# A hybrid encoder block on one core: two copies ahead of two subtractions, denser side steps at the end of the gates, a later Silu

## The chip, the cores and the metric

The kernel runs on one core of a Trainium2 chip. A core has five engines that the text speaks of: TensorE (PE in the profile, with PEld for its weight loads), VectorE (DVE), ScalarE (ACT), GpSimd (POOL) and SyncE (SP), which here issues nearly all DMAs. Each engine works off its own instruction queue strictly in order, and semaphores hold an instruction until what it needs is there. So an instruction that waits also holds everything that stands behind it on its engine. The metric is the time of one execution in microseconds of device time.

## The reference

The reference is one layer of a bidirectional hybrid encoder, with 1024 tokens of width 1024, all in fp32. What the change touches is in these lines, where `h` is the normalised input:

```python
proj = h @ w_in[l]
q, k, v, r, lr_f, lr_b, u, g_a, g_b = jnp.split(proj, split_points, axis=-1)
...
y_a = o @ w_branch_gla[l]            # o: gated linear attention of q, k, v, times silu(r)
...
merged = jax.nn.sigmoid(g_a) * y_a + jax.nn.sigmoid(g_b) * y_b     # y_b: pooling mixer of u
x = x + merged @ w_out[l]
h2 = rmsnorm(x, norm_ffn[l])
gate, up = jnp.split(h2 @ w_ffn_in[l], 2, axis=-1)
x = x + (jax.nn.silu(gate) * up) @ w_ffn_out[l]
```

## The kernel before

**Products.** Every fp32 operand is split into a high part (an fp32r cast by ACT) and a low part (what the cast lost, a subtraction on DVE or POOL). A product of one 128 by 512 tile and one k-tile is three matmuls: high with high, high with low, low with high (`products`, L268, and `mm3`, L273). The larger multiplications (the merge gates, branch and output projections, the FFN) are done in blocks of two by two with seven products in place of eight, so many sums and differences of blocks are formed first and split afterwards. One such product, in the gates and in the FFN, is twelve matmuls in a row into one bank of PSUM.

**The order of work** is written out by hand. The program issues TensorE's work in its order, and after each `mm3` calls `pump`, which counts the matmul time issued in units of one `mm3` of 512 columns and lets side work into the queues when its time has come:
- `soon(delay, step)` puts a step off by `delay` units;
- weights (`Ahead`, `Weights`) are split four products ahead: the cast `wh` on ACT (L197) and the low part `wl` on POOL (L198);
- `prepare_beside(jobs, every, put, lag)` takes a list of small jobs and does one step of it every `every` units. A step forms a sum or a difference on POOL (L636), casts the piece of an earlier step on ACT (`uph`, L630), subtracts for the piece before that on DVE (`upl`, L621), and puts the finished pair to DRAM on SP (L617). `finish_beside()` works off all steps that are left, at once. The `uph` and `upl` come from a ring of five buffers, so a cast waits until an earlier put has landed.

**The stages**, by the times of the trace: norms and the first transposes with the values of a pair of heads (to about 45 us); the first queries and keys and the attention of the four heads (to about 385); the merge gates (`Gates`, ten runs n = 0 to 9, to about 585); the branch projection, the merged projection (to 745); the FFN, whose first products run while the second half of the normalised input is still being transposed (`features(1)`, 744 to 788); FFN units and the output product (to 1381).

Three places matter here:
- `pair_products` (L440) forms the values of two heads at a time. A PSUM bank holds 256 columns for each head, and each half is split into `vh` and `vl`.
- At run n == 7 of the gates the side job is the splitting of the weights of the first two FFN units (`unit_jobs`, L563, two units, `READY`). In each of the last runs the pooled values of a group (`ph`, `pl`) are loaded (`load_pooled`, L1240) for the pooled product `yb`. The copies `ga` (ACT, L1308) take a finished product out of its bank, which TensorE needs again later.
- `features(half)` (L1525) transposes the normalised input, scales it into `hb` (ACT, L1540), and forms differences (DVE, L1554 and L1557) that are split into `gh` (ACT, `cast_block`, L1517) and `gl` (`low_block`, L1521, on DVE or POOL). Meanwhile `Gated.run` takes in the first gate products; for the first units the Silu of the gate is put off with `soon`.

Of the kernel before, what the change touches and what calls it, by code (L numbers as in the profile page):

```python
# [15 lines left out]
ALU = mybir.AluOpType  # L16
# [9 lines left out]
DV = 256  # L26
# [25 lines left out]
def kernel(  # L52
# [20 lines left out]
    nc = tc.nc  # L73
# [36 lines left out]
    def as_f32(ap):  # L110
        return ap.bitcast(F32)
# [39 lines left out]
    def soon(delay, *steps):  # L151
        put_off.extend([delay, step] for step in steps)
# [43 lines left out]
    def split_to(hi, lo, src, eng=nc.vector):  # L196
        nc.scalar.copy(hi, src)  # L197
        eng.tensor_tensor(lo, src, as_f32(hi), op=ALU.subtract)  # L198
# [239 lines left out]
    pair_v = [[], []]  # L438

    def pair_products(ts, before=None):  # L440
        banks = [bank(ps_mm) for _ in ts]
        for k in range(KT):
            if before:
                before(k)
            for ps, t in zip(banks, ts):
                mm3(ps[:, :], tokens(hT(k, t // 4), t), pair_w[k], k == 0, k == KT - 1)
        for ps, t in zip(banks, ts):
            for h in range(2):
                if t // 4 == len(pair_v[h]):
                    pair_v[h].append((slot(F32R, (4, DV), "vh"), slot(F32R, (4, DV), "vl")))  # L450
                split_to(*(part[:, t % 4, :] for part in pair_v[h][t // 4]), ps[:, h * DV : (h + 1) * DV])

    def first_steps(k):
        if k % 2 == 0:
# [68 lines left out]
    READY = 2  # L523
# [120 lines left out]
    def prepare_beside(jobs, every, put=PUT, lag=1):  # L644
        aside.append([beside(chain(*jobs), every, put, lag), every])

    def finish_beside():
        while aside:
            for _ in aside[0][0]:
                pass  # L650
            aside.pop(0)
# [250 lines left out]
    for h in range(HEADS):  # L902
# [7 lines left out]
        if h > 1:  # L910
            v = value_slots()
# [5 lines left out]
    class Unit:  # L917
# [14 lines left out]
        def block(self, i, j):  # L932
            return self.raw[i][:, 4 * j : 4 * j + 4, :]
# [227 lines left out]
    def load_block(i, j):  # L1161

        ob[i, j] = [slot(s="ob") for _ in range(2)]
        for c in range(2):
            nc.sync.dma_start(ob[i, j][c][:, :, :], ob_out[i, 1 - j][:, 2 * c : 2 * c + 2, :])
# [74 lines left out]
    def load_pooled(g):  # L1240

        while g not in stored and side:
            if next(side[0][0], None) is None:
                side.pop(0)
        if g not in stored:
            settle()
        pools[g] = [slot(F32R, s=s) for s in ("ph", "pl")]
        for n, t in enumerate(pools[g]):
            nc.sync.dma_start(as_f32(t[:, :, :]), p_out[g][n])
# [99 lines left out]
    for n, run in enumerate(gate_runs):  # L1349
        zs[n] = Gates(n)  # L1350
        last = n == len(gate_units) - 1
        if n == 0:
            prepare_beside(map(output_jobs, range(4)), 2.8)
        if n == 7:
            finish_side()
            finish_beside()
            prepare_beside(map(unit_jobs, range(READY)), 3.1, 1, 2)
        if last:
            finish_beside()
        for at, (of, p) in enumerate(run):  # L1360
            if not gates_ahead.step() and at in (5, 7):
                line_make()
            if n >= 6 and at == 2 and not last:
                load_pooled(n - 6)
            zs[of].run(p)
            for _ in range(2 * (at == 0 and not last)):
                gunits[n + 1].load()
            if p in (7, 4):
                zs[of].store(int(p == 4))
            if at == 4:  # L1370
                flush()
                if n == 2:
                    begin(pooling(), 4)
            if 5 <= n < 9 and at == 5:
                load_pool_weights(n - 5)
            elif n >= 6 and at == 2:
                split_pool_weights(n - 6)
            if n >= 6 and at == 0 and last:
                load_pooled(n - 6)
            if last and at == 1:  # L1380
                load_block(0, 0)
                line_load()
                line_load()
                load_block(1, 0)
            elif last and at == 2:
                line_load()
                line_load()
                load_block(0, 1)
                load_block(1, 1)
# [129 lines left out]
    def low_block(p, i, src, eng=nc.vector):  # L1519
        hi, lo = split_b[p][i]  # L1520
        eng.tensor_tensor(lo[:, :, :], src, as_f32(hi[:, :, :]), op=ALU.subtract)  # L1521
        if i == 1:
            split_done.add(p)

    def features(half):  # L1525

        for i in range(2):
            blocks[i, half] = [slot(s="hb") for _ in range(2)]

        def block(i, j, c):  # L1530
            return blocks[i, j][c][:, :, :]

        waiting = []
        for k in range(KT):
            ps = bank(ps_g, "tr")
            for i in range(4):
                nc.tensor.transpose(
                    ps[:, i * P : (i + 1) * P], xn[4 * half + i][:, k * P : (k + 1) * P], ident[:, :]
                )
            nc.scalar.activation(  # L1540
                blocks[k // 4, half][k % 4 // 2][:, k % 2, :], ps[:, :], AF.Copy, scale=g_ffn[:, k : k + 1]
            )
            if waiting:
                waiting.pop()()
            i = k % 4 // 2
            if k % 2 and half == 0:
                p, src = (1, block(0, 0, i)) if k < 4 else (2, block(1, 0, i))
                cast_block(p, i, src)
                low_block(p, i, src, nc.gpsimd)
            elif k % 2:  # L1550

                t = block(0, 0, i)
                if k < 4:
                    sub(t, block(0, 1, i), t)  # L1554
                    waiting.append(partial(cast_block, 5, i, t))
                else:
                    sub(t, block(1, 1, i), t)  # L1557
                    waiting.append(partial(cast_block, 6, i, t))
                    if k == KT - 1:
                        waiting.pop()()  # L1560
            elif half and k in (2, 4):
                low_block(5, k // 2 - 1, block(0, 0, k // 2 - 1), nc.gpsimd)
            elif half and k == 6:
                low_block(6, 0, block(0, 0, 0))
            yield 2 if half == 0 else 1.6 if k % 2 else 1.2
        if half == 0:
            return

        low_block(6, 1, block(0, 0, 1))
        for i in range(2):  # L1570
            cast_block(3, i, block(1, 1, i))
            yield 2.5
        for p, b in ((7, block(0, 1, 0)), (7, block(0, 1, 1)), (4, block(1, 0, 0)), (4, block(1, 0, 1))):
            i = len(split_b.get(p, ()))
            if p == 7:
                low_block(3, i, block(1, 1, i))
                sub(b, block(1, 1, i), b)
            else:
                low_block(7, i, block(0, 1, i))
                sub(b, b, block(0, 0, i))  # L1580
            cast_block(p, i, b)
            yield 3.5
        for i in range(2):
            low_block(4, i, block(1, 0, i))
# [70 lines left out]
    class Gated:  # L1655
# [15 lines left out]
        def run(self, p):  # L1671
            ps = bank_of(self, p)
            product(self.unit, p, ps, split_b)
            self.done.add(p)
            ps = ps[:, :]
            mul = partial(nc.vector.tensor_tensor, op=ALU.mult)
            if p == 1:
                self.sg = self.g[:, 0, :] if self.g else t2(s="sg")[:, :]
                nc.scalar.copy(self.sg, ps)  # L1679
            elif p == 2:  # L1680
                add(self.sg, ps, self.sg)  # L1681
                silu = partial(nc.scalar.activation, self.sg, self.sg, AF.Silu)
                if self.g:
                    soon(1, silu)
                else:
                    silu()
            elif p == 6:
                nc.scalar.copy(self.gate, ps)
            elif p == 5:
                nc.scalar.copy(self.up, ps)  # L1690
            elif p == 7:
                add(self.up, ps, self.up)
            elif p == 3:
                add(self.gate, ps, self.gate)
                nc.scalar.activation(self.gate, self.gate, AF.Silu)
            else:
                self.g = self.g or slot(s="g")
                mul(self.g[:, 0, :], ps, self.sg)
            if p in (3, 7) and {3, 7} <= self.done:
                self.g = self.g or slot(s="g")  # L1700
                mul(self.g[:, 1, :], self.gate, self.up)
# [255 lines left out]
```

## Time and profile before

| | us |
|---|---|
| median of 3 runs | 1389.14 |
| lowest and highest run | 1387.99, 1391.54 |
| profiled execution | 1389.97 |
| its span in the trace | 1388.2 |
| mean granted clock of TensorE | 0.998 |

By stage, the busy time of each engine, as the view by windows gives it:

| window | PE | DVE | ACT | POOL | DMA share |
|---|---|---|---|---|---|
| 0 to 40 | 32.16 | 25.50 | 26.64 | 13.95 | 0.58 |
| 40 to 140 | 98.67 | 46.94 | 52.22 | 24.76 | 0.17 |
| 140 to 385 | 243.95 | 159.00 | 141.08 | 90.01 | 0.31 |
| 385 to 585 | 197.72 | 126.91 | 89.60 | 133.98 | 0.79 |
| 745 to 788 | 40.38 | 26.33 | 24.89 | 10.27 | 0.47 |
| 788 to 1185 | 397.00 | 234.72 | 140.49 | 266.08 | 0.53 |
| 1185 to 1388.2 | 196.26 | 93.78 | 84.61 | 101.39 | 0.60 |

A row of the timeline reads: start, duration, engine, line, operation, what it writes and what it reads, shapes, how many such instructions in a row (x), and in brackets how long the engine had been idle before it and what ended that. Names are those of the tiles without buffer numbers. In the rows of the grouped waits the numbers are total idle time, how many times, and the longest.

### The profile page before, as it was taken

The numbers are of one execution on the slowest core, as the hardware profiler recorded it, in microseconds if no ns is written. First come the engines' busy times: TensorE is split into PE (matmuls) and PEld (weight loads), VectorE is DVE, ScalarE is ACT, GpSimd is POOL, SyncE is SP. The second block draws the span as 40 slices with busy tenths as digits, with TensorE's granted clock in tenths as the row PEclk, the third lists the DMA queues.
The fourth block names the chain that finished last, engine by engine and source line by source line (L and its number), as shares of the span: only waits on it lengthen the run. The fifth ranks groups of instructions, "written<-read, shape, count | busy, mean of one in ns | idle before, by whom it ended". The sixth has DMA issues, their size and how long they took to land. (4 is left out here: it accounts for less than half of the span.)

```text
span 1388.2 us, 18151 instructions
## 1 busy us (share of the span) xinstructions
PE 1366.0 (98%) x6485; PEld 1142.5 (82%) x6485; DVE 837.0 (60%) x1017; ACT 642.4 (46%) x1168; POOL 754.7 (54%) x557
## 2 busy tenths in 40 slices
PE   7999999999999999999999999999999999999997
PEld 6788898988888888788888788888888888888886
DVE  6364656557745875687883866565565556343374
ACT  6465766654334444554347533333333334444352
POOL 3222617132288645668665276666766667455453
PEclk9999999999999999999999999999999999999999
DMA  6112413312478677996516355555444447975551
GB/s 224 31 50 58 138 57 127 110 56 77 136 222 282 199 230 231 370 406 221 190 61 242 109 180 174 174 175 172 140 143 145 143 152 266 381 298 187 173 212 76
DMA packets 166586, 243.60 MB, mean 175 GB/s; under 512 B 10936, under 2 KB 95968, under 8 KB 166496
## 3 DMA queue, kind: packets, MB, share of 16 engines
q1 hardware_dynamic: 166352, 242.18, 51.6%
q8 instruction: 51, 0.84, 0.2%
q14 instruction: 39, 0.32, 0.1%
q10 hardware_dynamic: 144, 0.26, 0.0%
HBM read 164.55 MB, written 77.86 MB: 175 GB/s over the span
## 5 line engine op out<-in xcount | busy, mean ns | idle before, releaser
L198 POOL TENSOR_TENSOR wl<-fs,wh 128x512 fp32r<-128x512 f32 x120 | 167.1, 1396 | 149.5 <-ACT wh L197 100.4
L271 PE MATMUL ps<-gh,wh 128*128 128x512 f32 x616 | 240.7, 391 | 1.5 <-ACT gh L1517 0.8
L271 PE MATMUL ps<-gl,wh 128*128 128x512 f32 x616 | 240.0, 390 | 0.9 <-DVE gl L1521 0.9
L271 PE MATMUL ps<-gh,wl 128*128 128x512 f32 x616 | 239.7, 389 | 0.0
L198 POOL TENSOR_TENSOR wl<-fraw,wh 128x512 fp32r<-128x512 f32 x90 | 128.5, 1428 | 63.9 <-ACT wh L197 61.0
L271 PE MATMUL ps<-hh,wh 128*128 128x512 f32 x376 | 151.8, 404 | 0.0
L198 POOL TENSOR_TENSOR ol<-gor,oh 128x1024 fp32r<-128x1024 f32 (+1 forms) x42 | 101.0, 2408 | 86.4 <-ACT oh L197 62.0
L271 PE MATMUL ps<-hh,wl 128*128 128x512 f32 x376 | 146.9, 391 | 0.6 <-POOL wl L198 0.6
L271 PE MATMUL ps<-hl,wh 128*128 128x512 f32 x376 | 146.6, 390 | 0.0
L271 PEld LDWEIGHTS ps<-gh,wh 128*128 128x128 f32 x616 | 115.7, 188 | 26.4 <-ACT gh L1517 1.2
L271 PEld LDWEIGHTS ps<-gl,wh 128*128 128x128 f32 x616 | 115.7, 188 | 25.5 <-DVE gl L1521 1.6
L271 PEld LDWEIGHTS ps<-gh,wl 128*128 128x128 f32 x616 | 115.7, 188 | 24.0
L271 PE MATMUL ps<-oh,oh 128*128 128x512 f32 x308 | 119.8, 389 | 0.0
L271 PE MATMUL ps<-ol,oh 128*128 128x512 f32 x308 | 119.8, 389 | 0.0
L271 PE MATMUL ps<-oh,ol 128*128 128x512 f32 x308 | 119.8, 389 | 0.0
L198 POOL TENSOR_TENSOR wl<-raw,wh 128x512 fp32r<-128x512 f32 x40 | 54.5, 1373 | 118.2 <-ACT wh L197 109.6
L198 POOL TENSOR_TENSOR wl<-wraw,wh 128x512 fp32r<-128x512 f32 x56 | 91.9, 1672 | 42.3 <-ACT wh L197 39.4
L198 DVE TENSOR_TENSOR ol<-wor,oh 128x1024 fp32r<-128x1024 f32 (+1 forms) x42 | 61.9, 1486 | 66.9 <-ACT oh L197 54.3
L197 ACT CAST wh<-fs 128x512 fp32r<-128x512 f32 x120 | 73.8, 615 | 29.3 <-DVE fs L937 28.3
L271 PEld LDWEIGHTS ps<-hh,wl 128*128 128x128 f32 x376 | 70.6, 188 | 16.1 <-POOL wl L198 1.1
L271 PEld LDWEIGHTS ps<-hh,wh 128*128 128x128 f32 x376 | 70.7, 188 | 13.4 <-ACT wh L197 0.5
L271 PEld LDWEIGHTS ps<-hl,wh 128*128 128x128 f32 x376 | 70.8, 188 | 12.9
(259 smaller groups left out, 3120.9 us busy)
## 6 DMA issues: line engine op xcount, KB each, us to landing
fraw<-in_w_ffn_in_dram SPq DMA_DIRECT2D x44, 512.0 KB, 6.0
gor<-g_out SPq DMA_DIRECT2D x35, 512.0 KB, 5.0
g_out<-s SPq DMA_DIRECT2D x44, 256.0 KB, 2.3
raw<-in_w_in_dram SPq DMA_DIRECT2D x40, 256.0 KB, 4.8
fraw<-in_w_in_dram SPq DMA_DIRECT2D x20, 512.0 KB, 6.6
wor<-t_out SPq DMA_DIRECT2D x20, 512.0 KB
g_out<-g SPq DMA_DIRECT2D x33, 256.0 KB, 2.3
x<-in_x_dram SPq DMA_DIRECT2D x16, 512.0 KB, 4.1
```

The costliest lines, as they stand in the source:

```text
L197: nc.scalar.copy(hi, src)
L198: eng.tensor_tensor(lo, src, as_f32(hi), op=ALU.subtract)
L271: nc.tensor.matmul(ps, a[i], b[j], start=first and n == 0, stop=last and n == 2, skip_group_check=onto)
```

## The change

It has five parts, and TensorE's own order stays as it was.
1. `pair_products`: for each bank both heads' high parts are cast first, and then both low parts are formed. On each engine the order stays as it was, but the second cast no longer stands behind the first subtraction.
2. The side steps that split the first two FFN units' weights come every 2.8 units in place of 3.1.
3. What is left of them is worked off after the second product of the last gate run, not before its first.
4. `load_pooled` for the runs before the last comes after the third product of the run instead of ahead of it.
5. In `features(1)` the second low part of block 5 is formed on DVE and not on POOL, and the Silu of the gate products that run meanwhile is put off by four units in place of one.

```diff
@@ pair_products
-                split_to(*(part[:, t % 4, :] for part in pair_v[h][t // 4]), ps[:, h * DV : (h + 1) * DV])
+            parts = [[part[:, t % 4, :] for part in v[t // 4]] for v in pair_v]
+            halves = [ps[:, h * DV : (h + 1) * DV] for h in range(2)]
+            for (hi, _), src in zip(parts, halves):
+                nc.scalar.copy(hi, src)
+            for (hi, lo), src in zip(parts, halves):
+                nc.vector.tensor_tensor(lo, src, as_f32(hi), op=ALU.subtract)
@@ the loop over the gate runs
-            prepare_beside(map(unit_jobs, range(READY)), 3.1, 1, 2)
-        if last:
-            finish_beside()
+            prepare_beside(map(unit_jobs, range(READY)), 2.8, 1, 2)
         for at, (of, p) in enumerate(run):
...
-            if n >= 6 and at == 2 and not last:
-                load_pooled(n - 6)
             zs[of].run(p)
...
-            if n >= 6 and at == 0 and last:
+            if n >= 6 and at == (0 if last else 2):
                 load_pooled(n - 6)
             if last and at == 1:
+                finish_beside()
                 load_block(0, 0)
@@ features
             elif half and k in (2, 4):
-                low_block(5, k // 2 - 1, block(0, 0, k // 2 - 1), nc.gpsimd)
+                low_block(5, k // 2 - 1, block(0, 0, k // 2 - 1), (nc.gpsimd, nc.vector)[k // 2 - 1])
@@ Gated.run
                 if self.g:
-                    soon(1, silu)
+                    soon(4, silu)
```

**The pairs, on ACT.** The first bank of a later pair, with each instruction's waits (the name is the engine whose semaphore is waited for). Before:

```order
L685 ACTIVATE z_117_772<-z_117_772 128x512 [waits Activation_49]
L197 CAST vh_119_793<-ps_110_744 128x256 [waits PE_49]
L197 CAST vh_121_797<-ps_110_744 128x256 [waits DVE_49]
L691 ACT_TABLE_LOAD
L691 ACTIVATE z_111_748<-z_111_748 128x512 [waits Activation_49]
```

And after:

```order
L690 ACTIVATE z_117_772<-z_117_772 128x512 [waits Activation_49]
L454 CAST vh_119_793<-ps_110_744 128x256 [waits PE_49]
L454 CAST vh_121_795<-ps_110_744 128x256
L696 ACT_TABLE_LOAD
L696 ACTIVATE z_111_748<-z_111_748 128x512 [waits Activation_49]
```

The rows stand in the same order; the second cast of the bank has lost its wait for DVE.

**The end of the gates, on ACT.** From the last sum of run n = 8 to the first copies of the last run. Before:

```order
L1316 ACTIVATE ga_1047_5351<-ga_1047_5351 128x512
L630 CAST uph_1078_5503<-fraw_1036_5307 128x512
L630 CAST uph_1081_5514<-fraw_1035_5306 128x512
L630 CAST uph_1083_5520<-fraw_1035_5306 128x512
L197 CAST wh_1085_5528<-fraw_1040_5324 128x512
L1308 COPY ga_1089_5550<-ps_1088_5534 128x512
L197 CAST wh_1092_5556<-fs_1087_5532 128x512
```

And after:

```order
L1321 ACTIVATE ga_1047_5356<-ga_1047_5356 128x512
L635 CAST uph_1081_5512<-fraw_1030_5286 128x512
L197 CAST wh_1085_5523<-fraw_1042_5330 128x512
L1313 COPY ga_1089_5550<-ps_1088_5529 128x512
L197 CAST wh_1092_5556<-fs_1087_5527 128x512
```

Two of the three casts that stood directly ahead of the copy have moved to places between the products before it. The ones that were first have moved too, further up in the queue. Before:

```order
L1308 COPY ga_1047_5351<-ps_1044_5332 128x512
L197 CAST wh_1048_5353<-fraw_993_5116 128x512
L1316 ACTIVATE ga_997_5135<-ps_988_5092 128x512
L197 CAST wph_1054_5385<-wpr_1021_5244 128x256
L197 CAST wh_1056_5389<-fs_1050_5357 128x512
L1308 COPY ga_1039_5322<-ps_1034_5296 128x512
L197 CAST wh_1058_5407<-fraw_1040_5324 128x512
L630 CAST uph_1062_5417<-fraw_1036_5307 128x512
L630 CAST uph_1064_5430<-fraw_1035_5306 128x512
```

And after:

```order
L1313 COPY ga_1047_5356<-ps_1046_5338 128x512
L197 CAST wh_1048_5358<-fraw_993_5116 128x512
L1321 ACTIVATE ga_997_5135<-ps_988_5092 128x512
L635 CAST uph_1052_5381<-fraw_1031_5287 128x512
L197 CAST wph_1054_5384<-wpr_1021_5244 128x256
L197 CAST wh_1058_5392<-fs_1050_5362 128x512
L635 CAST uph_1060_5406<-fraw_1030_5286 128x512
L1313 COPY ga_1041_5328<-ps_1038_5306 128x512
```

Two `uph` casts that stood behind the copy of run n = 8 now stand ahead of it.

**The start of the FFN, on ACT.** `g_1439` is the first gate product; `hb_1458` to `hb_1461` are blocks of the second half. Before:

```order
L1517 CAST gh_1465_7259<-hb_1397_6967 128x1024
L162 ACT_TABLE_LOAD
L162 ACTIVATE g_1439_7151<-g_1439_7151 128x512
L1540 ACTIVATE hb_1459_7231<-tr_1470_7276,cols_173 128x512
L1540 ACTIVATE hb_1460_7232<-tr_1471_7286,cols_173 128x512
L1517 CAST gh_1472_7292<-hb_1398_6968 128x1024
L1540 ACTIVATE hb_1460_7232<-tr_1474_7299,cols_173 128x512
```

And after:

```order
L1519 CAST gh_1465_7259<-hb_1397_6967 128x1024
L1542 ACTIVATE hb_1459_7231<-tr_1470_7275,cols_173 128x512
L1542 ACTIVATE hb_1460_7232<-tr_1471_7285,cols_173 128x512
L1519 CAST gh_1472_7291<-hb_1398_6968 128x1024
L162 ACT_TABLE_LOAD
L162 ACTIVATE g_1439_7151<-g_1439_7151 128x512
L1542 ACTIVATE hb_1460_7232<-tr_1474_7299,cols_173 128x512
```

The table load and the Silu have moved behind two `hb` and one `gh`, and now stand directly ahead of the second half of `hb_1460`.

## The prediction

> **What bounds the kernel now.** I read the busy times first, then the waits of TensorE grouped by releaser, and then the timeline of each engine around TensorE's stops that the change can reach. The page's first part gives the bound.
>
> ```profile
> PE 1366.0 (98%) x6485; PEld 1142.5 (82%) x6485; DVE 837.0 (60%) x1017; ACT 642.4 (46%) x1168; POOL 754.7 (54%) x557
> ```
>
> TensorE is idle for only 1388.2 - 1366.0 = 22.2 us, so no change of order can bring more than that. The grouped waits of TensorE (total, times, longest) say where some of it lies:
>
> ```profile
> PE vps L428 <- DMA rows<-in_b_decay_bwd_dram: 6.6, 1, 6.6
> PE ps L271 <- ACT ga L1308: 2.3, 2, 1.6
> PE ps L271 <- DVE gl L1521: 0.9, 2, 0.8
> PE ps L271 <- POOL wl L198: 0.8, 2, 0.6
> ```
>
> The first 6.6 us are the load of the first rows, which the diff leaves alone. The other three name producers that the diff moves. These idle times understate the loss, because a matmul after a stop has nothing to overlap with. The ordinary cadence is (575.24 - 572.75) / 11 = 0.226 us:
>
> ```profile
> 572.75 0.39 PE L271 MATMUL ps<-hh,wh 128*128 128x512 f32 x1
> 575.24 0.39 PE L271 MATMUL ps<-hh,wl 128*128 128x512 f32 x1
> ```
>
> A row of 0.39 us every 0.226 us shows 0.17 us of overlap, which an idle engine loses; and the stopped matmul itself shows 0.50 us in place of 0.39. So each stop costs its bracketed idle time plus about 0.28 us, and one that shows 0.50 without a bracket about 0.28 us as well.
>
> **Part 1, the pair products: the second high copy goes ahead of the first subtraction.** Nothing is added or removed; ACT and DVE run the same rows. What goes is ACT's wait for DVE in front of each bank's second `vh`. Here ACT, then POOL, then TensorE:
>
> ```profile
> 43.64 0.37 ACT L197 CAST vh<-ps 128x256 fp32r<-128x256 f32 x1 [2.62 <-DVE vl L198]
> 45.81 2.35 ACT L325 ACTIVATE hh<-tr,cols 128x256 fp32r<-128x256 f32 x6
> 47.96 1.23 ACT L197 CAST wh<-raw 128x512 fp32r<-128x512 f32 x2
> 48.75 2.53 POOL L198 TENSOR_TENSOR wl<-raw,wh 128x512 fp32r<-128x512 f32 x2 [6.68 <-ACT wh L197]
> 44.66 0.60 PE L318 MATMUL tr<-ident,xn 128*128 128x128 f32 x4
> 48.72 0.50 PE L271 MATMUL ps<-hh,wh 128*128 128x512 f32 x1
> 50.08 0.50 PE L271 MATMUL ps<-hh,wl 128*128 128x512 f32 x1 [0.63 <-POOL wl L198]
> ```
>
> ACT stood 2.62 us, since DVE was in a row of `hl` work. Behind it in ACT's queue are ten `hh` and then `wh`; TensorE stops twice for `wh` and its `wl`, at 48.72 (0.28) and 50.08 (0.63 + 0.28), together 1.2 us. Without the stand ACT cannot gain the whole 2.62: the last two `hh` need the transposes that begin at 44.66 and end at 45.26, so they start about 45.4 and end 0.78 later (2.35 / 6 x 2), and `wh` starts near 46.2, 1.76 us earlier. POOL's first `wl` then ends near 48.2, before TensorE asks for it at about 49 (50.08 less the two stops' 1.2). Gain: 1.2 us. Its bounds are 0 (POOL held by something else in those 6.68 us) and 2.2 (if an attention stop of about a microsecond further on moves too). The price on DVE is that its first `vl` now waits for ACT's second copy, one `vh` of 0.37 us; DVE has 40% of the span free, so I cost that at nothing.
>
> **Parts 2 to 4, the end of the gates: steps of 2.8 units in place of 3.1, the remainder drained after the second product of the last run, the pooled load behind its product.** ACT's queue, with the put chain on DVE and SP, and TensorE:
>
> ```profile
> 549.23 0.59 ACT L1308 COPY ga<-ps 128x512 f32<-128x512 f32 x1 [0.55 <-PE ps L271]
> 557.75 0.62 ACT L630 CAST uph<-fraw 128x512 fp32r<-128x512 f32 x1 [6.08 <-DMA u_out<-upl]
> 566.97 0.62 ACT L630 CAST uph<-fraw 128x512 fp32r<-128x512 f32 x1 [1.77 <-DMA u_out<-upl]
> 568.22 0.62 ACT L630 CAST uph<-fraw 128x512 fp32r<-128x512 f32 x1 [0.63 <-POOL fraw L636]
> 569.26 0.58 ACT L1308 COPY ga<-ps 128x512 f32<-128x512 f32 x1
> 550.45 1.80 DVE L621 TENSOR_TENSOR upl<-fraw,uph 128x512 fp32r<-128x512 f32 x1 [5.04 <-ACT wh L197]
> 552.28 0.32 SPq L1249 DMA_DIRECT2D pl<-p_out  x1
> 554.47 0.39 PE L271 MATMUL ps<-trh,wh 128*128 128x512 f32 x1
> 557.42 0.39 PE L271 MATMUL yb<-pl,wph 128*128 128x512 f32 x1
> 569.89 0.50 PE L271 MATMUL ps<-trh,wh 128*128 128x512 f32 x1 [1.57 <-ACT ga L1308]
> 576.34 0.50 PE L271 MATMUL ps<-trh,wh 128*128 128x512 f32 x1 [0.71 <-ACT ga L1308]
> ```
>
> The drain writes its last casts `uph` into ACT's queue ahead of the copy that frees a bank of PSUM. They stand 1.77 and 0.63 us, the copy runs at 569.26, and TensorE waits for it: 1.57 + 0.28 = 1.85; the next copy, two products later, costs 0.71 + 0.28 = 0.99. Together 2.8 us.
>
> With the change a step comes every 2.8 units, and a unit is three matmuls, 0.68 us: 1.9 us in place of 2.1. Two units of three load steps and seven pieces, and four steps that carry the last piece through, make 24 steps or 67 units (74 before). The runs n = 7 and 8 with their pooled products offer 64 and the last run's first two products 8 more: nothing is left to drain, where before some three steps were. On SP the two puts of each piece are now issued ahead of loads behind which they stood, so the chain that held DVE for 5.04 us starts earlier. Followed through the queues with the durations above, ACT's last `uph` ends near 565, and the copy, started near 565.5, is done 2 us before TensorE needs its bank at 568.1 (569.89 less 1.85 and a margin for the signal). The second copy follows freely. Gain: 2.8 us. The lower bound is 0, if the casts still wait on landings; what would make it less than nothing is the slow rival below. The pooled load (ph, pl) moves behind a product and past four puts. Before, `pl` was issued at 552.28 and used at 557.42, 5.1 us later; its new place in SP's queue comes near 549, earlier than that, so I cost it at nothing. If the cover went, that is if those puts stayed at their times (the last near 555), a load of the same 5.1 us would stop TensorE for 555.6 + 5.1 - 557.4 = 3.3 us.
>
> **Part 5, the start of the FFN: the first Silu put off from one unit to four, one low part from POOL to DVE.** TensorE, ACT, DVE and POOL:
>
> ```profile
> 765.53 0.50 PE L271 MATMUL ps<-gh,wh 128*128 128x512 f32 x1 [0.44 <-ACT hb L1540]
> 767.40 0.50 PE L271 MATMUL ps<-gl,wh 128*128 128x512 f32 x1
> 769.09 0.50 PE L271 MATMUL ps<-gh,wh 128*128 128x512 f32 x1 [0.27 <-DVE g L1681]
> 772.52 0.50 PE L271 MATMUL ps<-gl,wh 128*128 128x512 f32 x1 [0.15 <-DVE gl L1521]
> 774.74 0.50 PE L271 MATMUL ps<-gh,wh 128*128 128x512 f32 x1 [0.79 <-ACT gh L1517]
> 776.00 0.50 PE L271 MATMUL ps<-gl,wh 128*128 128x512 f32 x1 [0.76 <-DVE gl L1521]
> 758.98 1.05 ACT L1517 CAST gh<-hb 128x1024 fp32r<-128x1024 f32 x1 [0.71 <-DVE hb L1554]
> 760.05 1.28 ACT L162 ACT_TABLE_LOAD   x1
> 761.35 0.63 ACT L162 ACTIVATE g<-g 128x512 f32<-128x512 f32 x1
> 763.85 1.05 ACT L1517 CAST gh<-hb 128x1024 fp32r<-128x1024 f32 x1 [0.71 <-DVE hb L1554]
> 762.59 1.22 DVE L1554 TENSOR_TENSOR hb<-hb,hb 128x1024 f32<-128x1024 f32 x1 [3.04 <-ACT hb L1540]
> 765.58 2.85 DVE L1557 TENSOR_TENSOR hb<-hb,hb 128x1024 f32<-128x1024 f32 x1 [1.77 <-ACT hb L1540]
> 760.11 2.39 POOL L1521 TENSOR_TENSOR gl<-hb,gh 128x1024 fp32r<-128x1024 f32 x1 [3.13 <-ACT gh L1517]
> 764.97 2.38 POOL L1521 TENSOR_TENSOR gl<-hb,gh 128x1024 fp32r<-128x1024 f32 x1 [2.47 <-ACT gh L1517]
> ```
>
> TensorE's six stops cost 0.72 + 0.28 + 0.55 + 0.43 + 1.07 + 1.04 = 4.1 us, a little less where two adjoin: 4.0. The same subtraction takes DVE 1.22 us alone and 2.85 beside POOL's `gl`, ending 1.08 us after POOL does (768.43 against 767.35); POOL's second `gl` is what holds the later ones up. After the change the table load and the Silu (1.9 us) stand behind the second `gh`. ACT reaches the `hb` that feeds the second subtraction at 760.1 and not at 761.9, but DVE can then begin at 760.8, beside POOL's first `gl` (760.11 to 762.50). By the row of 2.85 it ends near 763.5. The second `gh` follows to 764.65, the table load to 765.95, the Silu to 766.6, the next `hb` to 767.15: TensorE's stop of 765.53 moves to about 767.2, where it would have been ready at 764.92. That loses 2.25 + 0.11 = 2.4 us. But POOL's second `gl` is now DVE's (1.22 in place of 2.38, and nothing beside it), the third `gh` comes near 768.5, and TensorE, 1.7 us later, finds its operands: the five later stops go. Net 4.0 - 2.4 = 1.6, say 1.7 us. The upper bound takes the subtraction as unhindered, 1.22 us: `hb` at 765.5, a loss of 0.6, a gain of 3.4. The lower bound is 0: the 4.0 us only gather at one place. I take the middle, for the row of 2.85 is the same instruction beside the same neighbour.
>
> The Trainium skill ("ScalarE: Activation LUTs", What ACT_TABLE_LOAD costs) gives about 1283 ns for the load, as the row of 1.28 has it, and a drain of some 1380 ns more for each switch. This trace shows no such drain: the load begins 0.02 us after the cast ends, and the Silu 0.02 us after the load. By the page the stop would be 1.38 us longer, this part worth 0.3 us and the time 1385.3; since the trace is against it, its chance is 0.03, and it would end as the partial rival does.
>
> **The sum.** 1.2 + 2.8 + 1.7 = 5.7 us. Some of what is won early can be lost to a later producer that does not come earlier. The nearest row:
>
> ```profile
> 692.12 0.50 PE L271 MATMUL ps<-wl,dh 128*128 128x512 f32 x1 [0.18 <-POOL wl L198]
> ```
>
> There TensorE already meets POOL; I take back 0.5 us (0.18 + 0.28), between nothing and the 2.8 won just ahead of it. Left: 5.2 us. The profiled execution took 1389.97 us (span 1388.2 and 1.8 around it), 0.83 above the median of the runs, 1389.14. Against its own time that makes 1384.8, against the median 1389.14 - 5.2 = 1383.9, so 1384.0.
>
> **Rivals.** *Only part of it comes through.* The gates' stops go, the FFN's gather at one place and POOL takes back what the pairs won: 1389.14 - 2.8 + 0.5 = 1386.8. For it speaks that ACT's table load still stands ahead of an `hb` for which TensorE waits; against it, that five of the six stops name producers which become earlier.
>
> *More comes.* DVE's subtraction runs unhindered and nothing is given back: 1.2 + 2.8 + 3.4 = 7.4, so 1381.7. The row of 2.85 speaks against it.
>
> *The denser steps turn into a wait, and it is slower.* The casts share five buffers with their low parts, so each waits for a put to land; ACT stood 6.08 us on one. In the new order such a cast stands ahead of the copy of 549.23, where before it stood behind. That copy frees the bank for TensorE at 554.47, so it can slip by 4.6 us (554.47 - 549.23 - 0.6). A stand like the old one, 6.08, costs 1.5 + 0.3, less than the rest wins. From 4.6 + 5.2 = 9.8 us on it decides; twice the old stand, 12.2, costs 12.2 - 4.6 = 7.6 and makes 1389.14 - 5.2 + 7.6 = 1391.5. Against it: the puts go earlier on SP, ahead of the loads that delayed them.
>
> *Nothing happens in the pairs,* because the order on each engine is the same and something other than that wait holds `wh`: 1385.2.
>
> **Chances.** The sum as it stands 0.45, more 0.13, nothing in the pairs 0.1, part of it 0.2, slower 0.12. What this kernel's measurement can tell from no change is about 0.3%, 4.2 us, so "faster" ends at 1385.0. The forecast with its spread of about 1.5 us lies mostly below (0.4 of 0.45), "more" wholly, the pairs' rival about half: 0.58. "Same" takes the rest of these and the partial case: 0.31. Slower 0.11. The range runs from the "more" case to just short of no change, 1381.3 to 1388.4; what is left out is mostly the slow case. The likeliest one's own range is 1382.5 to 1385.5.
>
> **What would show it.** In the profile after: no idle time of ACT ahead of the second `vh` of a bank, and no TensorE stop at 48 to 51; no row of TensorE waiting for `ga`, or one under 0.5 us; the last `uph` ahead of the copies by 2 us; one stop of some 2 us for `hb` near 763 (all times there come about 4 us earlier) with the table load just ahead of it, and none for `gl` or `gh` after it. The prediction is wrong if ACT's idle time ahead of the `uph` casts grows, if `yb` waits for `pl`, or if TensorE's waits for POOL's `wl` grow by what the others lose.

## The result, and the profile after

| | median us | lowest to highest | ratio to before |
|---|---|---|---|
| before | 1389.83 (6 runs) | 1387.99 to 1391.54 | |
| changed | 1383.67 (6 runs) | 1382.08 to 1384.79 | 0.9954, interval 0.9941 to 0.9967 |

The changed kernel is 0.46% faster, 6.2 us by the medians. The profiled execution took 1382.44 us, with a span of 1380.4, so the two profiled executions lie 7.5 us apart, and their spans 7.8. Of the kinds of stops of TensorE that remain, its grouped waits show these, in the same columns as before (two kinds of one stop of 0.2 us each are left out):

```profile
PE vps L428 <- DMA rows<-in_b_decay_bwd_dram: 6.6, 1, 6.6
PE ps L271 <- ACT hb L1542: 2.3, 1, 2.3
PE op L271 <- DVE p L198: 0.4, 2, 0.2
PE tr L318 <- DVE xn L307: 0.3, 1, 0.3
PE ps L271 <- POOL wl L198: 0.2, 1, 0.2
```

The rows for `ga`, `gl` and `gh` are gone, the one for `wl` has shrunk from 0.8 to 0.2, and one stop for `hb` of 2.3 us stands where one of 0.4 us was. (Lines behind L451 of the old kernel have moved by five lines, those behind the gate runs by two.)

The pairs, on ACT, POOL and TensorE, where before the second `vh` stood 2.62 us and TensorE stopped twice:

```profile
37.34 0.68 ACT L454 CAST vh<-ps 128x256 fp32r<-128x256 f32 x2
44.50 0.84 ACT L325 ACTIVATE hh<-tr,cols 128x256 fp32r<-128x256 f32 x2 [0.29 <-PE tr L318]
45.23 1.14 ACT L197 CAST wh<-raw 128x512 fp32r<-128x512 f32 x2
45.92 2.55 POOL L198 TENSOR_TENSOR wl<-raw,wh 128x512 fp32r<-128x512 f32 x2 [7.12 <-ACT wh L197]
48.20 0.39 PE L271 MATMUL ps<-hh,wl 128*128 128x512 f32 x1
```

The two `vh` run back to back, `hh` is held by the transposes alone, and the matmul that stopped for `wl` runs without a stop. The end of the gates, in the same way:

```profile
557.69 0.62 ACT L635 CAST uph<-fraw 128x512 fp32r<-128x512 f32 x1 [3.17 <-DMA u_out<-upl]
561.62 0.62 ACT L635 CAST uph<-fraw 128x512 fp32r<-128x512 f32 x1 [0.30 <-DMA u_out<-upl]
562.67 0.58 ACT L1313 COPY ga<-ps 128x512 f32<-128x512 f32 x1
546.10 0.56 SPq L1254 DMA_DIRECT2D pl<-p_out  x1
564.44 0.39 PE L271 MATMUL ps<-trh,wh 128*128 128x512 f32 x1
```

The last `uph` ends at 562.24, the copy at 563.25, and TensorE goes from `yb` into the next product at 564.44 without a stop. The casts still wait for landings (3.17 us once), but in places where nothing is urgent behind them. The pooled load is issued at 546.10, 6 us earlier than before, of which about 3.8 us are the lead that TensorE has by then. The start of the FFN:

```profile
753.46 2.40 POOL L1523 TENSOR_TENSOR gl<-hb,gh 128x1024 fp32r<-128x1024 f32 x1 [3.14 <-ACT gh L1519]
754.00 2.94 DVE L1556 TENSOR_TENSOR hb<-hb,hb 128x1024 f32<-128x1024 f32 x1 [1.10 <-ACT hb L1542]
756.98 1.05 ACT L1519 CAST gh<-hb 128x1024 fp32r<-128x1024 f32 x1 [2.42 <-DVE hb L1556]
758.04 1.28 ACT L162 ACT_TABLE_LOAD   x1
759.34 0.63 ACT L162 ACTIVATE g<-g 128x512 f32<-128x512 f32 x1
760.59 0.51 PE L271 MATMUL ps<-gh,wh 128*128 128x512 f32 x1 [2.30 <-ACT hb L1542]
```

This is the chain of the prediction row by row: the subtraction beside POOL's `gl`, the cast, the table load, the Silu, `hb`, TensorE.

**Where the time went.** TensorE's order is the same in both kernels and in all experiments below, so the time between the same two matmuls can be compared. This table gives it as a difference to the trace of before; the columns are named by the times of before.

| | 7 to 25 | 25 to 60 | 108 to 135 | 135 to 300 | 560 to 590 | 755 to 785 | 785 to 800 |
|---|---|---|---|---|---|---|---|
| changed | -0.91 | -1.19 | -1.19 | -0.41 | -2.86 | -1.60 | +0.45 |
| e1_pairs | +0.26 | -1.21 | -1.19 | -0.55 | -0.16 | +1.65 | 0.00 |
| e2_gates | 0.00 | -0.02 | -0.01 | +0.24 | -2.86 | +0.01 | 0.00 |
| e3_ffn | -0.38 | -0.02 | -0.01 | -1.27 | -0.03 | -0.11 | 0.00 |
| e4_silu | -0.83 | 0.00 | -0.01 | -0.13 | +0.07 | -1.60 | 0.00 |
| e5_low | -0.99 | -0.02 | 0.00 | -0.57 | -0.03 | -1.14 | 0.00 |
| e6_finish | -0.02 | -0.01 | 0.00 | -0.70 | -0.47 | +1.65 | 0.00 |
| e7_dense | -0.74 | -0.02 | -0.03 | -0.43 | -2.86 | +1.63 | 0.00 |
| x1_twolow | -0.72 | -1.19 | -1.19 | -0.63 | -2.86 | -2.26 | 0.00 |
| x2_table | +0.14 | -1.24 | -1.19 | -0.22 | -2.86 | -3.02 | 0.00 |
| x3_both | -0.49 | -1.24 | -1.19 | -0.29 | -2.72 | -3.62 | 0.00 |
| x4_low_silu | 0.00 | -1.24 | -1.19 | -1.00 | -2.87 | -3.04 | 0.00 |
| x5_all | +0.03 | -1.24 | -1.19 | -1.22 | -2.86 | -3.60 | 0.00 |

Four columns answer to an edit and repeat within 0.2 us wherever that edit is made (the +1.6 at 755 to 785 apart, of which the last section tells). The columns 7 to 25 and 135 to 300 differ with no regard to the edits: they differ from one execution to the next. The 0.45 us at 785 to 800, a wait for a weight from DRAM, stands in the one trace of the changed kernel and in no other.

### The profile page after: what moved, and what is told of

Read it like the earlier page. It is cut to its first block, busy times and chain, and to the rows that moved or that the text cites. A ratio compares the mean times of both kernels' runs of the same rounds, so it can differ in the third digit from the quotient of the medians.

```text
span 1380.4 us, 18150 instructions
## 1 busy us (share of the span) xinstructions
PE 1362.9 (99%) x6485; PEld 1142.9 (83%) x6485; DVE 834.8 (60%) x1018; ACT 642.3 (47%) x1168; POOL 751.6 (54%) x556
```

## The experiments

**Each of the change's places alone.** On the kernel before, part 1 only; the new lines of `pair_products` as in the diff above:

```diff
-                split_to(*(part[:, t % 4, :] for part in pair_v[h][t // 4]), ps[:, h * DV : (h + 1) * DV])
...
+            for (hi, _), src in zip(parts, halves):
+                nc.scalar.copy(hi, src)
+            for (hi, lo), src in zip(parts, halves):
+                nc.vector.tensor_tensor(lo, src, as_f32(hi), op=ALU.subtract)
```

> Part 1 alone, on the kernel before. Theory: the second vh of a bank no longer stands, wh is cast 1.8 us earlier, and TensorE's two stops at 48.7 and 50.1 go (1.2 us by the prediction; 1.0 in the trace after, before the one at 111, where another 1.0 went), so 1.2 to 2.3 us less than before, and the stops of the gates and of the FFN stay as they were (2.8 and 4.0). Rival: the order on each engine is unchanged, so nothing happens here, and what the trace after won before 115 us (3.2 us, of which 1.05 at 20.7, ahead of the first instruction that the change touches) is the difference of two executions: then within 0.5 us of before.

Measured: 1387.58 against 1390.53 us, ratio 0.998 (0.9971 to 0.9989). The two stops at 48.7 and 50.1 are gone (-1.21), and so are two in the attention (-1.19). The rows of TensorE there, before:

```profile
111.15 0.38 PE L271 MATMUL op<-vh,p 128*128 128x256 f32 x1 [0.44 <-ACT p L197]
111.87 0.39 PE L271 MATMUL op<-vh,p 128*128 128x256 f32 x1 [0.22 <-DVE p L198]
```

and with part 1 alone:

```profile
109.62 0.28 PE L271 MATMUL op<-vh,p 128*128 128x256 f32 x1
109.86 0.28 PE L271 MATMUL op<-vh,p 128*128 128x256 f32 x1
```

Between the pairs and this place ACT had stood for the same reason as at 43.64. In the kernel before:

```profile
96.31 0.65 ACT L197 CAST vh<-ps 128x256 fp32r<-128x256 f32 x2 [3.57 <-DVE vl L198]
97.51 0.37 ACT L197 CAST vh<-ps 128x256 fp32r<-128x256 f32 x1 [0.55 <-DVE vl L198]
```

After these two stands of 3.57 and 0.55 us, ACT's casts `p` came late to TensorE. Part 1 is worth 2.4 us by the trace. The rival, that nothing happens, falls.

Parts 2 to 4 only (the spacing, the moved drain, the moved pooled load, as in the diff):

> Parts 2 to 4 alone, on the kernel before. Theory: the two stops for the copies at the end of the gates go, 2.6 to 2.8 us less than before; the stops at 48.7, 50.1 and 111 stay, and the FFN's start keeps its six. Rival: part of it is given back at POOL's low parts in the projections behind the gates (0.5 to 1 us), so 1.8 to 2.3. If the stop at 20.7 for DVE's hl is here as in before, it is a matter of the program; if it is there in some runs only, it is a difference between executions.

Measured: 1387.69 against 1390.53 us, ratio 0.9977 (0.9968 to 0.9986), and -2.86 us between 560 and 590. Nothing is given back in the projections behind. The stop at 20.7 stands here as in before, while it is shorter in other experiments that do not touch it either: a difference between executions.

Part 5 only:

> Part 5 alone, on the kernel before. Theory: one stop of about 2.3 us for hb in place of six with 4.0 together, so 1.7 us less than before, with DVE's second subtraction taking about 2.9 us beside POOL's gl. Rival: it is given back at the weights that come from DRAM just behind (0.3 us in the trace after at 788.8), so 1.4 or less.

Measured: 1388.05 against 1390.53 us, ratio 0.9985 (0.9975 to 0.9994). The six stops are replaced by one of 2.28 us; the trace shows only -0.11 because a spell of half clock that costs about 1.5 us falls on this stage in this execution (below). The wait at 788.8 does not show here, nor in any other experiment, so it was no price of part 5.

**Which half of part 5.** The Silu alone:

```diff
-                    soon(1, silu)
+                    soon(4, silu)
```

> The Silu put off by four units, POOL keeping both low parts, on the kernel before. Theory: the stop for hb grows to about 2.3 us as with all of part 5, and POOL's second gl (2.4 us, ready only behind the second gh) still makes the next subtraction on DVE long; the four stops for g, gl and gh shrink but do not all go: TensorE's loss between 760 and 778 about 3 to 3.5 us against 4.0. Rival: the put-off alone does it all, 2.4 us.

One execution: 1387.80 us beside one of 1388.46 of the kernel before; a single pair decides little, so this run and the next three are read from their traces. The rival holds: -1.60 us between 755 and 785, the same as with both edits. The trace, TensorE, DVE and POOL:

```profile
766.65 0.50 PE L271 MATMUL ps<-gh,wh 128*128 128x512 f32 x1 [2.29 <-ACT hb L1540]
766.70 1.22 DVE L1557 TENSOR_TENSOR hb<-hb,hb 128x1024 f32<-128x1024 f32 x1 [3.70 <-ACT hb L1540]
764.16 2.35 POOL L1521 TENSOR_TENSOR gl<-hb,gh 128x1024 fp32r<-128x1024 f32 x1 [2.24 <-ACT gh L1517]
```

POOL's second `gl` now runs from 764.16 to 766.51, while ACT loads the table and does the Silu, and it is over when DVE's next subtraction starts. So that subtraction takes 1.22 us in place of 2.85 with POOL's `gl` still there. The put-off moved the two apart.

The low part alone:

```diff
-                low_block(5, k // 2 - 1, block(0, 0, k // 2 - 1), nc.gpsimd)
+                low_block(5, k // 2 - 1, block(0, 0, k // 2 - 1), (nc.gpsimd, nc.vector)[k // 2 - 1])
```

> One low part on DVE, the Silu put off by one unit as before, on the kernel before. Theory: the first stop for hb (0.7 us) stays, gl is ready 1.2 us earlier and DVE's next subtraction takes 1.22 in place of 2.85 us, so the four later stops shrink by most of their 3 us: TensorE's loss between 760 and 778 about 1 to 1.5 us, less than with both edits, and the put-off would be the half that costs. Rival: the chain through ACT (table load and Silu ahead of the second gh) keeps them late whatever DVE does, and about 3 us stay.

One execution: 1387.57 us beside 1388.46; -1.14 us between 755 and 785. The rival holds: of the 4.0 us, 2.9 stay. Three of the six stops are as long as before, those for `hb` and for the last `gh` and `gl`:

```profile
764.22 0.50 PE L271 MATMUL ps<-gh,wh 128*128 128x512 f32 x1 [0.45 <-ACT hb L1540]
772.27 0.50 PE L271 MATMUL ps<-gh,wh 128*128 128x512 f32 x1 [0.78 <-ACT gh L1517]
773.53 0.50 PE L271 MATMUL ps<-gl,wh 128*128 128x512 f32 x1 [0.76 <-DVE gl L1521]
```

So each half is worth most of it alone, and the second adds nothing to the put-off: 1.60, 1.14, and both together 1.60.

**Which part of the gates' edits.** The drain moved, the spacing left at 3.1:

```diff
-        if last:
-            finish_beside()
@@
             if last and at == 1:
+                finish_beside()
                 load_block(0, 0)
```

> The steps stay at 3.1 units, only the drain is moved behind the second product of the last run, on the kernel before. Theory: the first copy has one late cast ahead of it where before it had three, so the first stop (1.85 us) shrinks to under 0.7; the second stays, as a cast now stands ahead of that copy: 0 to 1 us of the 2.8 is left as loss at each. Rival: the landings set the pace, and the first stop stays above 1.3 us.

One execution: 1391.30 us beside 1388.46, of which 1.65 is the cost of a spell of half clock. Both copies are in time, so the theory has the first stop and not the second; and a new one comes that neither named. TensorE, ACT and DVE:

```profile
582.19 0.50 PE L271 MATMUL ps<-trh,wh 128*128 128x512 f32 x1 [1.58 <-DVE ga L1313]
579.23 1.05 ACT L1152 CAST dh<-ob 128x1024 fp32r<-128x1024 f32 x1 [2.37 <-DMA ob<-ob_out]
580.31 1.23 DVE L162 TENSOR_TENSOR dl<-ob,dh 128x1024 fp32r<-128x1024 f32 x1 [4.12 <-ACT dh L1152]
581.45 0.68 DVE L1313 TENSOR_TENSOR ga<-ps,ga 128x512 f32<-128x512 f32 x1
```

On SP the loads of the blocks `ob` for the next stage stand right behind the drain; the first is issued at 573.95, where before it was issued at 571.15. DVE waits 4.12 us for what ACT casts of them, and the sum that frees a bank stands behind that. The gain of the copies is given back at 582 and a little later (-0.47 in all to 590, +0.66 to 755).

The spacing alone, with the drain and the pooled loads where they were:

```diff
-            prepare_beside(map(unit_jobs, range(READY)), 3.1, 1, 2)
+            prepare_beside(map(unit_jobs, range(READY)), 2.8, 1, 2)
```

> The steps at 2.8 units, the drain and the pooled loads where they were, on the kernel before. Theory: ACT's order around the copies is then the same as with all three edits, so the spacing alone takes both stops away (2.6 to 2.8 us), and the moved drain has nothing to do. Rival: the pooled loads, still issued ahead of the puts on SP, hold the put chain, and the casts stay late: a stop of 1 us or more remains for ga.

One execution: 1387.76 us beside 1388.46, with -2.86 us between 560 and 590, to the hundredth what all three edits give. The spacing carries the gates' gain; the moved drain and the moved pooled loads have no share in it that this trace shows. (This execution, too, has a spell, which costs 1.63 us.)

**What still holds the FFN's start.** All on the changed kernel. First, the other low part of block 5 on DVE as well:

```diff
-                low_block(5, k // 2 - 1, block(0, 0, k // 2 - 1), (nc.gpsimd, nc.vector)[k // 2 - 1])
+                low_block(5, k // 2 - 1, block(0, 0, k // 2 - 1), nc.vector)
```

> The changed kernel, with the first low part of block 5 on DVE too and not on POOL. Theory (POOL's gl is what stretches DVE's second subtraction from 1.22 to 2.94 us): DVE does gl in 1.22 us and the subtraction right behind in 1.22, which ends 1.1 us earlier; gh, table load, Silu and hb follow 1.1 us earlier, and TensorE's stop for hb shrinks from 2.3 to 1.2 us; 1.1 us less than the changed kernel, about 1382.5. Rival (the subtraction is long for another reason, such as its operands): it stays near 2.9 us, ends 1.2 us later than now behind the gl, and the stop grows to 3.5 us: 1.2 us more.

Measured: 1382.61 us, ratio to before 0.9938 (0.9926 to 0.995). DVE's rows:

```profile
753.60 1.22 DVE L1523 TENSOR_TENSOR gl<-hb,gh 128x1024 fp32r<-128x1024 f32 x1 [1.11 <-ACT gh L1519]
754.75 0.68 DVE L1683 TENSOR_TENSOR g<-ps,g 128x512 f32<-128x512 f32 x1
755.35 1.21 DVE L1556 TENSOR_TENSOR hb<-hb,hb 128x1024 f32<-128x1024 f32 x1
```

The subtraction takes 1.21 us once POOL has no `gl` beside it, in place of 2.94: the rival falls. It won 0.66 us and not 1.1, since the add `g` (0.68 us), which DVE did before the subtraction was ready, now stands between the two.

Second, the table loaded early:

```diff
     project(0, BRANCH, collect_branch, before_branch)
+    warm = vec(1, "warm")
+    nc.scalar.activation(warm[:, :], cols[:, :1], AF.Silu)
```

> The changed kernel, with a Silu of one column put in after the branch projection, so that the table is loaded there once and not in front of the first Silu of the FFN. Theory (the stop for hb is the end of a chain on ACT: gh, table load, Silu, hb): the chain loses 1.28 us, the stop shrinks from 2.3 to 1.0 us, about 1.3 us less than the changed kernel. Rival: ACT's 1.4 us in the merged projection delay a weight that TensorE needs (POOL's low parts met TensorE there at 692), and it is given back: within 0.5 us of the changed kernel.

Measured: 1381.52 us, ratio 0.9932 (0.9918 to 0.9946). The stop for `hb` falls from 2.30 to 0.88 us, -1.42 against the changed kernel in that stage, and nothing shows in the merged projection. The table load is worth its own row of 1.28 us and 0.14 more: with it the Silu begins 0.02 us after the load, and without it at 759.67, 0.10 us before the cast ahead of it has ended. The figure of the Trainium skill ("ScalarE: Activation LUTs", What ACT_TABLE_LOAD costs) with its drain would have made 2.66; no run here shows a drain at this place.

Third, both of these:

> The changed kernel with both: the first low part of block 5 on DVE, and the table loaded early. Theory: with POOL out of the way the stop was 1.72 us, and without the table load 0.45; 1.9 us less than the changed kernel, about 1381.3 to 1382. Rival: the parts that come from DRAM behind it (a wait of 0.15 us at 788.8 in the changed kernel) take back half or more: 1 us or less.

Measured: 1380.44 us, ratio 0.9926 (0.9912 to 0.994), which lies wholly below the interval of the changed kernel (0.9941 to 0.9967). TensorE's stop:

```profile
759.36 0.50 PE L271 MATMUL ps<-gh,wh 128*128 128x512 f32 x1 [0.31 <-ACT hb L1544]
```

That stage is 2.0 us shorter than in the changed kernel (-3.62 against -1.60). The theory's 0.45 us of stop were 0.31, and nothing was taken back.

Fourth and fifth, the low part with the Silu put off by five, and all three:

```diff
-                    soon(4, silu)
+                    soon(5, silu)
```

> The changed kernel with the first low part of block 5 on DVE and the Silu put off by five units, which sets the table load behind the hb for which TensorE waits, and ahead of the next hb. Theory: that stop falls from 1.72 to about 0, but the next hb, which is 1.9 us later in ACT's queue, holds DVE's next subtraction, gh and gl, so stops of up to 1.5 us for gl or gh come back some 5 us later: net 0.3 to 1.7 us less than with the low part alone. Rival: those have no slack at all, and nothing is won.

> All three on the changed kernel: both low parts on DVE, the table early, the Silu put off by five units. Theory: only 0.63 us of Silu is left in ACT's way and it stands behind the hb: no stop above 0.3 us from 755 to 780, 2.3 to 2.5 us less than the changed kernel, and not more than 0.5 us better than with the first two. Rival: the weights from DRAM become the bound at 788, and it is no better than those two.

Measured: 1381.06 us, 0.9931 (0.9918 to 0.9944), and 1380.67 us, 0.9928 (0.9915 to 0.9941). In the first the stop for `hb` is gone and one for `gl` has come:

```profile
766.79 0.50 PE L271 MATMUL ps<-gl,wh 128*128 128x512 f32 x1 [0.76 <-DVE gl L1523]
```

The work put behind the one `hb` delayed the next one, as its theory said, and the stage is 0.78 us shorter than with the low part alone (-3.04 and -2.26). With all three the theory's stops came out (one is left, of 0.28 us for `gl`), but not its time: the stage is as short as with two (-3.60 and -3.62), 2.0 us less than in the changed kernel in place of 2.3 to 2.5. The rival's outcome holds, and not the reason it gave, for nothing is lost at 785 to 800. So x3_both is the version to take: by the ratios 0.28% below the changed kernel and 0.74% below the one before.

## Why the prediction was right, point by point

The predicted 1384.0 us stood against 1383.67, and the direction and the range held. Its terms were 1.2 + 2.8 + 1.7 - 0.5, together 5.2; the traces give 2.4 + 2.9 + 1.6 - 0, which is 6.8 before rounding. So the mechanisms held, the gain was reckoned too small by 1.6 us, and the closeness of the time is in part luck. (The 22.2 us of idle time are no strict bound either: by the prediction's own count a stop costs about 0.28 us more than its idle time.)

**The pairs.** The mechanism held: the second `vh` no longer stands, `wh` begins at 45.23 with the TensorE stops gone; those at 48.7 and 50.1 were worth 1.2 us as reckoned. The term was too small by 1.2 us. The step that failed is the choice between its bounds: the attention's stops at 111 were named as an upper bound and left out of the value, and they went too. The row of 96.31, with 3.57 us of the same wait, stood in the trace before and was not quoted or followed.

**The end of the gates.** Predicted 2.8, measured 2.86. The casts were done ahead of the copy, though with less to spare than reckoned: the last `uph` ends 0.4 us before the copy begins, and the copy 1.2 us before TensorE goes on, where 2 us were named for each. The pooled load was issued earlier than before. Of the three edits that this term priced as one, the experiments leave the spacing alone as the cause; that the drain finds nothing left was the reason given, and with it the moved drain can do nothing.

**The start of the FFN.** Predicted 1.7 of a possible 0 to 3.4, measured 1.60; DVE's row of 2.94 beside POOL, the order of cast, table load and Silu, and the one stop of 2.3 us for `hb` came out as reckoned. The reason given for the later stops was wrong in part: they go with the put-off alone, POOL keeping its second `gl` (e4_silu), because that `gl` then runs while ACT is busy with the Silu. The low part on DVE, to which the prediction gave it, adds nothing on top.

**The part taken back.** 0.5 us, put at POOL's low parts in the projections. It was not there: TensorE's wait at 692 stayed at 0.2 us, and from 590 to 755 the changed kernel gains or loses 0.06 us.

**Why the time came out so near.** The term that was too small by 1.2 and the 0.5 us taken back for nothing err the same way, so they don't cancel: the four edited stages sum to 6.8 us (1.19 + 1.19 + 2.86 + 1.60) against the 5.2 predicted. Chance made up for 1.4 of these 1.6 us: the kernel before has a median of 1389.83 us over six runs where the prediction started from 1389.14 (0.7), and the medians show only 6.2 us of the 6.8 (another 0.7). The interval of the ratio, 4.6 to 8.2 us, holds both. Of the rivals, "nothing in the pairs" fell with e1_pairs, and "only part of it" with that and the -1.60 us at the start of the FFN, where it expected none; "more comes" needed DVE's second subtraction to run unhindered, and with the Silu put off it does so only where both low parts are on DVE (x1_twolow, x3_both, x4_low_silu, x5_all); the slow one met its condition nowhere, as the longest stand of a cast is 3.17 us.

## What to carry to other kernels

Where one engine is 98% busy, list its stops with what ended each, and follow every one back through the in-order queue of the engine that ended it: what stands there in front of the late instruction is the thing to move. Look for the same wait further on as well; here the stops at 111 went with those at 48. An edit that moves two instructions that hinder each other apart in time can replace one that takes the work off the engine, so try each half alone. What is loaded once, such as an activation table, belongs where its engine has time and not in front of the first use.

## What the runs showed of the hardware that was not expected

**Spells of half clock.** In four traces of fourteen (e1_pairs, e3_ffn, e6_finish, e7_dense) TensorE runs at half rate for about 3.4 us at the start of the FFN. In e1_pairs, TensorE's rows there and one row of the view by windows (the number after the busy times is the granted clock):

```profile
775.42 0.63 PE L271 MATMUL ps<-gh,wl 128*128 128x512 f32 x1
775.85 0.63 PE L271 MATMUL ps<-gh,wh 128*128 128x512 f32 x1
```

```profile
775.00:777.60 2.60, 2.60 (x8) 2.02 (x7) 2.60 (x3) 1.53 (x2) 0.00 (x0) 0.50 0.00 0
```

The matmuls start 0.43 us apart where they otherwise start 0.23 apart, at a granted clock of 0.50. The same view gives 0.80 for 774.0 to 774.5 and 0.86 for 777.6 to 778.0, so the half clock lasted from 774.3 to 777.7, 3.4 us. A spell costs 1.5 to 1.65 us. Each of the four begins 0.7 to 1.3 us after one of TensorE's stops. All four stand in kernels that keep the old stops of this stage or the one of 2.3 us, and none in the five with the stops shortened; but before, changed, e2_gates, e4_silu and e5_low have stops and no spell. That the stops bring them on is possible and not shown. They are a part of the spread between executions.

**A stop that a tenth of a microsecond decides.** TensorE's stop of 1.0 us at 20.7 was there before and is missing in the trace after, with the same instructions. In the kernel before, DVE and POOL:

```profile
18.46 1.29 POOL L198 TENSOR_TENSOR wv<-vraw,wv 128x512 fp32r<-128x512 f32 x1
18.52 1.77 DVE L307 TENSOR_SCALAR xn<-x,n1rs 128x1024 f32<-128x1024 f32 x1 [0.67 <-POOL n1rs L303]
```

and in the changed kernel:

```profile
18.74 0.75 DVE L307 TENSOR_SCALAR xn<-x,n1rs 128x1024 f32<-128x1024 f32 x1 [0.67 <-POOL n1rs L303]
18.81 1.83 POOL L198 TENSOR_TENSOR wv<-vraw,wv 128x512 fp32r<-128x512 f32 x1
```

The two start within 0.1 us of each other. Whichever starts first takes its normal time (POOL 1.29, DVE 0.75), and the other takes 0.5 to 1.1 us longer; so it is in thirteen of the fourteen traces, and in e1_pairs, where the starts lie 0.01 us apart, DVE is the one held up. TensorE then waits 0.4 to 1.1 us where DVE is held up (seven traces), and at most 0.2 us where it isn't. This agrees with the Trainium skill ("SBUF — State Buffer", Who interferes with whom), by which DVE and GpSimd share a pair of ports that one of them holds alone. So two executions of the same instructions can differ here by about a microsecond.
